# Meta tokens' state update as one product of stacked parts, retention keys in three pieces, and refills two products later, in a hybrid retention and attention block

## The chip, the cores and the metric
One core of a Trainium2 chip runs the kernel. The metric is device time in microseconds of one execution, as the median of the runs. TensorE is called PE, VectorE DVE, ScalarE ACT, GpSimd POOL and SyncE SP.

## The reference
A single encoder block on 1024 tokens of 1024 channels. Sixteen learned meta tokens go in front, so T = 1040. After an RMS norm one product with `w_in` gives the inputs of two branches and their gates:

```python
rq = _rotary(rq); rk = _rotary(rk) * RET_DK ** -0.5        # 4 heads of 128
o_r = _bidirectional_retention(rq, rk, rv, lg_f, lg_b)       # rv: 4 heads of 256
o_r = groupnorm(o_r) * ret_nw * silu(rg);  y_r = o_r @ w_rb
o_a = _windowed_sink_attention(rotary(aq), rotary(ak), av, sink)   # 8 heads, 2 groups
y_a = (o_a * silu(ag)) @ w_ab
mix = sigmoid(gr) * y_r + sigmoid(ga) * y_a
out = h + rms_norm(mix @ w_o)                               # meta tokens dropped
```

Retention works in chunks of 128 tokens. For a chunk c of one head, in one direction:

```python
inner = (q k^T * decay) v                      # inside the chunk
cross = (q * q_decay) @ state                  # what came before
state = chunk_decay * state + (k * k_decay)^T v
```

The meta tokens are a short chunk 0 of 16 tokens: only their state update is needed, in the forward direction.

## The kernel before
**Numbers.** All is in float32 quality: an operand is split into a high and a low part (`..h` and `..l`, of type fp32r), and `mm3` forms a product as three matmuls, high by high (line 76), low by high (77) and high by low (78), summed in one PSUM bank. ACT or POOL copies out the high part, DVE subtracts (`dve_lo`, line 92). The transposed, split input lies in `big`.

**PSUM.** Eight banks in four tags: `pj` has three (projections), `p1` two (transposes `tr` of keys, transposes `to` of outputs), `p2` two (state updates `pkv`), `p3` one (outputs `pa` forward, `pb` backward).

**Setup** (0 to 40 us): the input comes in tile by tile, and the products of head 0 (keys `pk0`, queries `pq0`) follow it in `qk0_mm`. `evac_qk0` rotates them (`rope_evac`: three DVE operations and one POOL addition for each piece).

**Retention** (40 to 330 us), heads 0 to 3. `gen_qk(h)` makes the keys and queries of a head: keys in four `PIECES` of 272, 256, 256, 256 columns, queries in two `HALVES` of 512, each by `proj` (8 k-tiles of `mm3`), then `rope_late` (two DVE multiplications, and two DMAs of POOL that add the swapped halves). It is a generator that yields after each k-tile, so that other code can draw from it by `fill(n)`. `retention(h)` goes over the chunks twice:
- the forward scan: `stage1(c)` projects the values (`pv`, 24 matmuls of 256), splits them into `vh`, `vl` (four buffers each), transposes the keys and forms the scores (tile `tr`), and scales the transposed keys into `khf`, `klf` (forward) and `khb`, `klb` (backward); `stage2(c)` forms the output `pa` (6 matmuls), which ACT and DVE bring to `op`, and the state updates `pkv`: the forward half is added into the state `Sf` on DVE, the backward half is kept by ACT in `kvb`. For chunk 0, all operands have 16 rows, and there is only the forward update, three matmuls of 16 rows.
- the backward scan: for each chunk from 8 to 1 the state `Sb` (DVE) is split (POOL, DVE), `pb` takes three matmuls, DVE adds it to `op` (line 619) and norms it over the 256 channels (lines 623 to 627); `finish` transposes it (`to`, line 595) and ACT copies it out scaled (`ost`, line 600). Between the chunks `fill(KT)` (8 steps) draws the next head's `gen_qk`, 7 times in a head, or in head 3 the keys and values of attention.

**Attention** (330 to 500 us, with the first weights of the later phases), then three **large products** in phases z, r and a: block products by a Strassen-like scheme (seven block products in z and r, with sums T1 to T4 of blocks of the right operand; in a, the sums come from DRAM). `refill` returns, for each numbered place between products, which loads and which splits of the next phase's right operand are issued there.

**Order.** Engines execute in order. The order of instructions is set by the tile scheduler, which takes the program's order and `issue_after` pins and lays the instructions of all engines by its own costs; pools give out buffers and banks in the order of the program.

Of the kernel before, what the change touches and what calls it, by code (L numbers as in the profile page):

```python
# [7 lines left out]
F32 = mybir.dt.float32  # L8
R = mybir.dt.float32r
# [12 lines left out]
SCALE = 128 ** -0.5  # L22
PIECES = [(0, 272), (272, 528), (528, 784), (784, 1040)]
HALVES = [(16, 528), (528, 1040)]
MW = 416
LEFT = 48
FILL = (9, 9, 7, 7, 7, 7, 6, 6), (7,) * 8, (7, 6, 6, 6, 6, 6, 6, 5), (5, 5, 5, 5, 5, 5, 8)
# [12 lines left out]
def block_kernel(ctx: ExitStack, tc: tile.TileContext, x0, xT, x, meta, w_in, w_rb, w_ab, w_out, post_w,  # L40
# [136 lines left out]
    cr = ra.tile([P, T], F32, name="cr")  # L177
    sr = ra.tile([P, T], F32, name="sr")

    def rope_late(t, a, b, o, nm):  # L180

        n = b - a
        m = ra.tile([P, 512], F32, tag="m", bufs=4, name=f"m_{nm}")
        nc.vector.tensor_tensor(m[:, 0:n], t[:, 0:n], sr[:, a:b], ALU.mult)
        nc.vector.tensor_tensor(o[:, 0:n], t[:, 0:n], cr[:, a:b], ALU.mult)
        for r in (0, 64):
            nc.gpsimd.dma_start(o[64 - r:128 - r, 0:n], m[r:r + 64, 0:n], accum_op=ALU.add)

    def rope_evac(t, a, b, o, nm):
        n = b - a  # L190
        m1, m2 = (ra.tile([P, 512], F32, tag="m", bufs=4, name=f"m{i}_{nm}") for i in (1, 2))
        nc.vector.tensor_tensor(m1[:, 0:n], t[:, 0:n], cr[:, a:b], ALU.mult)
        nc.vector.tensor_tensor(m2[64:128, 0:n], t[0:64, 0:n], sr[0:64, a:b], ALU.mult)
        rot = nc.vector.tensor_tensor(m2[0:64, 0:n], t[64:128, 0:n], sr[64:128, a:b], ALU.mult).ins
        nc.gpsimd.tensor_tensor(o[:, 0:n], m1[:, 0:n], m2[:, 0:n], ALU.add)
        return rot


# [53 lines left out]
    def evac_qk0(*pieces):  # L252
        if 0 not in qk:
            qk[0] = [], ra.tile([P, 4, 272], F32, tag="kp", bufs=2, name="kr0")
        q, kt = qk[0]
        for i in pieces:
            m0, a, b, t = (outs[2:] + outs[:2])[i]
            if m0:
                o = kt[:, i]
            else:  # L260
                o = ra.tile([P, 512], F32, tag="q", bufs=6, name=f"qr0_{i}")
                q.append(o)
            rot = rope_evac(t, a, b, o, f"qk0_{i}")
        return rot

    with tc.tile_pool(name="setup", bufs=1, reuse_waits="tile") as st:
# [46 lines left out]
            nc.tensor.matmul(idle[:, 0:KT * (32 + NM)], zeros[:, 0:P], zeros, start=True, stop=True)  # L313


        outs = [(P, a, b, t(f"pk0_{a}")) for (a, b), t in zip(PIECES, (pj, pj, p1, p3))]
        outs = [(0, a, b, p2(f"pq0_{a}")) for a, b in HALVES] + outs

        def qk0_mm(k):
# [53 lines left out]
        first = [projT(wv0, 0, "pv0_0", vmeta0), projT(wv0, 1, "pv0_1"), projT(wv0, 2, "pv0_2")]  # L373
    ra.tile([P, 32], F32, name="space_q")
    with tc.issue_after(rotated):
        turned = evac_qk0(4)
    with tc.issue_after(turned):
        nc.vector.memset(ms, 1.0)
        nc.vector.tensor_scalar(ms[0:NM, 0:1], sumsq[0:NM, 0:1], 1.0 / D, EPS, op0=ALU.mult, op1=ALU.add)
# [61 lines left out]
    def gen_qk(h):  # L441
        w = load_w(w_in, U_QK + h)
        q, kt = [], ra.tile([P, 4, 272], F32, tag="kp", bufs=2, name=f"kr{h}")
        qk[h] = (q, kt)
        for i, (a, b) in enumerate(PIECES):
            t = yield from proj(w, P, a, b, f"pk{h}_{i}")
            rope_late(t, a, b, kt[:, i], f"k{h}_{i}")
            yield
        for i, (a, b) in enumerate(HALVES):
            t = yield from proj(w, 0, a, b, f"pq{h}_{i}")  # L450
            o = ra.tile([P, 512], F32, tag="q", bufs=6, name=f"qr{h}_{i}")
            rope_late(t, a, b, o, f"q{h}_{i}")
            q.append(o)
            yield
# [3 lines left out]
    def retention(h, fill, begin=lambda: None):  # L458
# [21 lines left out]
        def stage1(c):  # L480
            n = NM if c == 0 else P
            pv = first.pop(0) if first else projT(wv, c, f"pv{h}_{c}", vmeta)
            vh = rp.tile([P, 256], R, tag="vh", bufs=4, name=f"vh{h}_{c}")
            vl = rp.tile([P, 256], R, tag="vl", bufs=4, name=f"vl{h}_{c}")
            state["v"] = nc.scalar.copy(vh[0:n], pv[0:n, 0:256]).ins
            state["vl"] = dve_lo(vl[0:n], pv[0:n, 0:256], vh[0:n])
            tr = (p2 if h and c < 2 else p1)(f"tr{h}_{c}")
            nc.tensor.transpose(tr[0:n, 0:P], ksl(c), ident)
            if c > 0:
                nc.tensor.matmul(tr[:, P:2 * P], ksl(c), qs(q, c), start=True, stop=True)  # L490
            kd = {}
            space("space_k", 16)
            for d in ("f", "b"):
                if d == "f" and c > 7 or d == "b" and c < 2:
                    continue
                sc = kd_(h, c, n) if d == "f" else kd_(NH + h, c, n)
                if d == "b":
                    space("space_b", 16)
                a = rp.tile([P, P], R, tag="kh" + d, bufs=2, name=f"kh{d}{h}_{c}")
                b = rp.tile([P, P], R, tag="kl" + d, bufs=2, name=f"kl{d}{h}_{c}")  # L500
                nc.scalar.activation(a[0:n], tr[0:n, 0:P], AF.Copy, scale=sc)
                nc.vector.scalar_tensor_tensor(b[0:n], tr[0:n, 0:P], sc, a[0:n].bitcast(F32), op0=ALU.mult,
                                               op1=ALU.subtract)
                kd[d] = (a, b)
            s = None
            if c > 0:
                sd = rp.tile([P, P], F32, tag="sd", bufs=3, name=f"sd{h}_{c}")
                a = rp.tile([P, P], R, tag="sh", bufs=3, name=f"sh{h}_{c}")
                b = rp.tile([P, P], R, tag="sl", bufs=3, name=f"sl{h}_{c}")
                nc.vector.scalar_tensor_tensor(sd, tr[:, P:2 * P], r2[:, c:c + 1], DT[:, h], op0=ALU.mult, op1=ALU.mult)  # L510
                nc.scalar.copy(a, sd)
                dve_lo(b, sd, a)
                s = (a, b)
            st1[c] = (n, vh, vl, kd, s)
# [9 lines left out]
        def stage2(c):  # L524
            n, vh, vl, kd, s = st1.pop(c)
            if c > 0:
                fh, fl = state["fs"]
                pa = p3(f"pa{h}_{c}")
                mm3(pa[:, 0:256], s[0], s[1], vh, vl, True, True)
                mm3(pa[:, 256:512], qs(qh, c), qs(ql, c), fh, fl, True, True)  # L530
                o = op[c - 1]
                nc.scalar.activation(o, pa[:, 0:256], AF.Copy, scale=rcol[:, c:c + 1])
                nc.vector.scalar_tensor_tensor(o, pa[:, 256:512], qdf(h, c), o, op0=ALU.mult, op1=ALU.add)
            if kd:
                pk = p2(f"pkv{h}_{c}")
            if "f" in kd:
                a, b = kd["f"]
                mm3(pk[:, 0:256], a[0:n], b[0:n], vh[0:n], vl[0:n], True, True)
                new = rp.tile([P, 256], F32, tag="S", bufs=2, name=f"Sf{h}_{c}")
                if c == 0:  # L540
                    nc.vector.tensor_copy(new, pk[:, 0:256])
                else:
                    nc.vector.scalar_tensor_tensor(new, state["f"], cdf(h), pk[:, 0:256], op0=ALU.mult, op1=ALU.add)
                state["f"] = new
                state["fs"] = split_state(new, f"f{h}_{c}")
            if "b" in kd:
                a, b = kd["b"]
                mm3(pk[:, 256:512], a, b, vh, vl, True, True)
                nc.scalar.copy(kvb[c - 1], pk[:, 256:512])
# [56 lines left out]
        for c in range(NB, 0, -1):  # L606
# [25 lines left out]
            if c < 8:  # L632
                with ExitStack() as behind:
                    for p in pins:
                        behind.enter_context(tc.issue_after(p))
                    fill(KT)
            if c == 1:
                begin()
            if c < NB - 1:
# [82 lines left out]
    def gen_ak(g, pieces_=range(4)):  # L722
        if not wak:
            wak.append(load_w(w_in, U_AK))
        for i in pieces_:
            a, b = PIECES[i]
            t = yield from proj(wak[0], P * g, a, b, f"pak{g}_{i}")
            o = rotated_k[g, i] = ra.tile([P, 272], F32, tag="ak", bufs=2, name=f"akr{g}_{i}")
            rope_late(t, a, b, o, f"ak{g}_{i}")
            if not g and i:  # L730
                keys(g, i - 1)
            yield
# [133 lines left out]
    with tc.issue_after(normed):  # L866
        evac_qk0(2)
        decay_table((0,))
        evac_qk0(3, 5)
    heads, drains = [], []  # L870

    def begin_head(h):
# [272 lines left out]
    def refill(nm, src):  # L1145
# [21 lines left out]
            return lambda: get_pre(n)  # L1167

        at = {-16: [load(0, 0)] + ([] if nm == "a" else [load(0, 1)]), -14: [load(1, 1)]}
        each(at, -13, split("B11", 0, 0))  # L1170
        if nm == "a":
            at.update({-11: [got("T1")], -10: [load(1, 0)], -9: [got("T2")], -5: [got("T3")], -1: [got("T4")]})
            each(at, -7, split("B21", 1, 0))
            each(at, -3, split("B22", 1, 1))
            return at
        each(at, -11, minus((0, 0), (0, 1), (0, 0)), split("T1", 0, 0))
        at[-10].append(load(1, 0, range(3)))
        each(at, -7, minus((0, 0), (1, 1), (0, 0)), split("T2", 0, 0))
        each(at, -3, split("B21", 1, 0), minus((0, 0), (1, 0), (0, 0)))
        at[-2].append(load(1, 0, (3,)))  # L1180
        at[1] = at.pop(0)
        each(at, 2, minus((0, 1), (1, 1), (0, 1)))
        each(at, 3, split("T3", 0, 1))
        each(at, 5, split("B22", 1, 1))
        each(at, 7, split("T4", 0, 0))
        return at

    def run(phases):
# [493 lines left out]
```

## Time and profile before
| | |
|---|---|
| median of 3 runs | 1040.86 us (1039.69 to 1041.02) |
| profiled execution | 1040.1 us, its span 1038.3 us |
| PE busy | 1023.7 us, 5883 matmuls |
| DVE busy | 835.8 us, 1802 instructions |
| ACT busy | 502.6 us |
| POOL busy | 228.0 us |
| clock granted to PE | 1.00 in all stretches |

The profile is of one execution. "Busy" is the time in which an engine has an instruction in work; consecutive matmuls overlap in their recorded lengths, so the cost of one in a full queue is the distance from its start to the next start. A view of stretches gives these times for parts of the span; a view of waits tells what an idle engine waited for. All of it is from the kernel before.

### The profile page before, as it was taken

How to read it: one execution, taken by the hardware profiler on the slowest of the kernel's cores; microseconds unless marked ns; L12 is line 12 of the kernel's file. 1: busy time of each engine (PE TensorE's matmuls, PEld its weight loads, DVE VectorE, ACT ScalarE, POOL GpSimd, SP SyncE). 2: the span in 40 equal slices, each digit the busy share in tenths (PEclk: the TensorE clock that was granted, in tenths of full speed). 3: DMA queues.
4: the chain of work that ended last, by engine and by line, in shares of the span. 5: the costliest groups of instructions: out<-in, count | busy, mean ns of one | idle time of the engine just before them, and what ended most of it. 6: DMA issues, size and time to landing. Idle time of an engine off the chain costs nothing. (4 is left out here: it accounts for less than half of the span.)

```text
span 1038.3 us, 17311 instructions
## 1 busy us (share of the span) xinstructions
PE 1023.7 (99%) x5883; PEld 898.0 (86%) x5883; DVE 835.8 (80%) x1802; ACT 502.6 (48%) x1129; POOL 228.0 (22%) x368
## 2 busy tenths in 40 slices
PE   9999999999999999999999999999999999999997
PEld 8998999989989888988888888878888788788886
DVE  7886758768875778778769989999899799778665
ACT  5531432423424566665667554455567446334442
POOL 3445244243342333444310000000000000111032
PEclk9999999999999999999999999999999999999999
DMA  9433123243241466675559679899935746789464
GB/s 357 164 87 88 65 47 84 78 88 104 78 93 62 103 182 189 175 188 161 168 176 326 209 260 338 294 330 365 373 102 178 252 153 226 231 231 325 127 122 81
DMA packets 98840, 188.45 MB, mean 181 GB/s; under 512 B 13024, under 2 KB 37632, under 8 KB 98192
## 3 DMA queue, kind: packets, MB, share of 16 engines
q1 hardware_dynamic: 81200, 162.89, 46.6%
q0 software_dynamic: 10176, 14.73, 9.6%
q10 hardware_dynamic: 7376, 9.73, 2.7%
q8 instruction: 46, 0.75, 0.3%
q14 instruction: 42, 0.34, 0.1%
HBM read 124.32 MB, written 57.68 MB: 175 GB/s over the span
## 5 line engine op out<-in xcount | busy, mean ns | idle before, releaser
L1286 POOL DMA_DIRECT2D mx_d<-c1a x4 | 3.6, 890 | 395.8 <-DVE c1a L1277 377.2
L77 PE MATMUL bz<-big,llz 128*128 128x512 f32 x192 | 74.8, 390 | 0.2 <-DVE llz L92 0.2
L78 PE MATMUL bz<-big,lhz 128*128 128x512 f32 x192 | 74.4, 389 | 0.0
L76 PE MATMUL bz<-big,lhz 128*128 128x512 f32 x192 | 74.0, 390 | 0.3 <-ACT lhz L978 0.3
L76 PE MATMUL pv<-wh,big 128*128 128x256 f32 x256 | 72.8, 284 | 0.0
L77 PE MATMUL pv<-wh,big 128*128 128x256 f32 x256 | 72.7, 284 | 0.0
L78 PE MATMUL pv<-wl,big 128*128 128x256 f32 x256 | 72.7, 284 | 0.0
L76 PE MATMUL bz<-T,lhz 128*128 128x512 f32 x176 | 68.1, 390 | 1.1 <-DVE u2z L1068 1.1
L78 PE MATMUL bz<-T,lhz 128*128 128x512 f32 x176 | 68.5, 389 | 0.0
L77 PE MATMUL bz<-T,llz 128*128 128x512 f32 x176 | 68.5, 389 | 0.0
L76 PE MATMUL paq<-big,wh 128*128 128x512 f32 x128 | 51.6, 403 | 0.0
L1426 ACT ACTIVATE p<-raw,nm 128x337 f32<-128x337 f32 (+1 forms) x64 | 35.5, 556 | 32.2 <-DVE nm L1423 30.6
L77 PE MATMUL paq<-big,wl 128*128 128x512 f32 x128 | 50.2, 392 | 0.0
L78 PE MATMUL paq<-big,wh 128*128 128x512 f32 x128 | 50.2, 392 | 0.0
L1439 POOL TENSOR_SCALAR p<-p,den 128x336 f32<-128x336 f32 (+2 forms) x60 | 34.6, 624 | 66.5 <-DVE den L1430 59.1
L76 PEld LDWEIGHTS pv<-wh,big 128*128 128x128 f32 x256 | 48.3, 189 | 0.4
L77 PEld LDWEIGHTS pv<-wh,big 128*128 128x128 f32 x256 | 48.3, 189 | 0.4
L78 PEld LDWEIGHTS pv<-wl,big 128*128 128x128 f32 x256 | 48.2, 188 | 0.3
L92 DVE TENSOR_TENSOR wl<-wr,wh 128x1024 fp32r<-128x1024 f32 x28 | 35.1, 1258 | 10.4 <-POOL wh L89 6.7
L76 PEld LDWEIGHTS bz<-big,lhz 128*128 128x128 f32 x192 | 36.1, 188 | 8.1 <-ACT lhz L978 0.7
L77 PEld LDWEIGHTS bz<-big,llz 128*128 128x128 f32 x192 | 36.0, 188 | 7.9 <-DVE llz L92 0.5
L78 PEld LDWEIGHTS bz<-big,lhz 128*128 128x128 f32 x192 | 36.0, 188 | 7.5
(621 smaller groups left out, 3594.6 us busy)
## 6 DMA issues: line engine op xcount, KB each, us to landing
wrz<-in_w_in_dram SPq DMA_DIRECT2D x32, 512.0 KB, 6.1
wr<-in_w_in_dram SPq DMA_DIRECT2D x29, 512.0 KB, 4.1
we<-in_w_in_dram SPq DMA_DIRECT2D x16, 512.0 KB, 4.3
tg<-tg_d SPq DMA_DIRECT2D x32, 256.0 KB, 5.1
e<-e ACTq DMA_DIRECT2D x20, 256.0 KB, 2.7
e<-e SPq DMA_DIRECT2D x20, 256.0 KB, 5.3
xn<-in_x_dram SPq DMA_DIRECT2D x8, 512.0 KB, 9.5
oTr_d<-ost SPq DMA_DIRECT2D x16, 256.0 KB, 2.1
```

The source lines that it names most:

```text
L76: nc.tensor.matmul(o, ah, bh, start=first, stop=False, **kw)
L77: nc.tensor.matmul(o, al, bh, start=False, stop=False, **kw)
L78: latest[:] = [nc.tensor.matmul(o, ah, bl, start=False, stop=last, **kw).ins]
L92: return nc.vector.tensor_tensor(o, i, hi.bitcast(F32), ALU.subtract).ins
L1286: nc.gpsimd.dma_start(d, to, accum_op=ALU.add)
L1426: last["exp"] = nc.scalar.activation(pp[:, x_, w0 - o:w0 - o + 1 + wid], r[:, 0:1 + wid], AF.Exp, scale=-1.0, bias=nm_[:, x_:x_ + 1], accu ...
L1439: nc.gpsimd.tensor_scalar(v, v, den[:, x_:x_ + 1], 1.0, op0=ALU.mult, op1=ALU.mult)
```

## The change
Three edits.

1. **Meta state update.** For chunk 0 there is no `vl` and `klf`. `vh` (128 x 256) is cleared by DVE and the 16 rows of the high part of the values are put at rows 0 and 32, the low part at row 64. `khf` (128 x 128) is cleared, and the high part of the keys put at rows 0 and 64, the low part at row 32. One matmul of 128 rows then sums the three products.
2. **Keys in three pieces.** `KEYS` has 272, 256 and 512 columns; the last piece is written to two slots of the key tile through a view of 2 x 256 (`key_piece`, `like`). In head 0 the setup holds one PSUM bank less for keys. The backward scan draws `(9, 5, 6, 6, 6, 8, 8)` steps instead of `8` each in heads 0 to 2, since the three pieces have 8 steps fewer; head 3 is as before. Attention's keys keep `PIECES`.
3. **Refills.** In phases z and r the places of the loads and splits are two products later, up to some that lie one later; phase a is unchanged.

```diff
+KEYS = [(0, 272), (272, 528), (528, 1040)]
...
+    def key_piece(t, i, n):
+        return t[:, 2:4, 0:256] if i == 2 else t[:, i, 0:n]
+
+    def like(t, o):
+        return t.rearrange("p (a c) -> p a c", a=2) if len(o.shape) > 2 else t
...
-        nc.vector.tensor_tensor(o[:, 0:n], t[:, 0:n], cr[:, a:b], ALU.mult)
+        nc.vector.tensor_tensor(o, like(t[:, 0:n], o), like(cr[:, a:b], o), ALU.mult)
         for r in (0, 64):
-            nc.gpsimd.dma_start(o[64 - r:128 - r, 0:n], m[r:r + 64, 0:n], accum_op=ALU.add)
+            nc.gpsimd.dma_start(o[64 - r:128 - r], like(m[r:r + 64, 0:n], o), accum_op=ALU.add)
...
-        outs = [(P, a, b, t(f"pk0_{a}")) for (a, b), t in zip(PIECES, (pj, pj, p1, p3))]
+        outs = [(P, a, b, t(f"pk0_{a}")) for (a, b), t in zip(KEYS, (pj, p1, p3))]
...
-        for i, (a, b) in enumerate(PIECES):
+        for i, (a, b) in enumerate(KEYS):
             t = yield from proj(w, P, a, b, f"pk{h}_{i}")
-            rope_late(t, a, b, kt[:, i], f"k{h}_{i}")
+            rope_late(t, a, b, key_piece(kt, i, b - a), f"k{h}_{i}")
...
-            vl = rp.tile([P, 256], R, tag="vl", bufs=4, name=f"vl{h}_{c}")
-            state["v"] = nc.scalar.copy(vh[0:n], pv[0:n, 0:256]).ins
-            state["vl"] = dve_lo(vl[0:n], pv[0:n, 0:256], vh[0:n])
+            if c:
+                vl = rp.tile([P, 256], R, tag="vl", bufs=4, name=f"vl{h}_{c}")
+                state["v"] = nc.scalar.copy(vh, pv[:, 0:256]).ins
+                state["vl"] = dve_lo(vl, pv[:, 0:256], vh)
+            else:
+                vl = None
+                nc.vector.memset(vh.bitcast(F32), 0.0)
+                for r in (0, 32):
+                    nc.scalar.copy(vh[r:r + n], pv)
+                dve_lo(vh[64:64 + n], pv, vh[0:n])
...
+                if not c:
+                    nc.vector.memset(a.bitcast(F32), 0.0)
+                    for r in (0, 64):
+                        nc.scalar.activation(a[r:r + n], tr[0:n, 0:P], AF.Copy, scale=sc)
+                    nc.vector.scalar_tensor_tensor(a[32:32 + n], tr[0:n, 0:P], sc, a[0:n].bitcast(F32), op0=ALU.mult,
+                                                   op1=ALU.subtract)
+                    kd[d] = a
+                    continue
...
-                a, b = kd["f"]
-                mm3(pk[:, 0:256], a[0:n], b[0:n], vh[0:n], vl[0:n], True, True)
+                if c:
+                    mm3(pk[:, 0:256], *kd["f"], vh, vl, True, True)
+                else:
+                    nc.tensor.matmul(pk[:, 0:256], kd["f"], vh, start=True, stop=True)
...
-                    fill(KT)
+                    fill(KT if h == NH - 1 else (9, 5, 6, 6, 6, 8, 8)[c - 1])
...
-        each(at, -13, split("B11", 0, 0))
+        each(at, -13 if nm == "a" else -11, split("B11", 0, 0))
...
-        each(at, -11, minus((0, 0), (0, 1), (0, 0)), split("T1", 0, 0))
-        at[-10].append(load(1, 0, range(3)))
-        each(at, -7, minus((0, 0), (1, 1), (0, 0)), split("T2", 0, 0))
-        each(at, -3, split("B21", 1, 0), minus((0, 0), (1, 0), (0, 0)))
-        at[-2].append(load(1, 0, (3,)))
-        at[1] = at.pop(0)
-        each(at, 2, minus((0, 1), (1, 1), (0, 1)))
-        each(at, 3, split("T3", 0, 1))
-        each(at, 5, split("B22", 1, 1))
-        each(at, 7, split("T4", 0, 0))
+        each(at, -9, minus((0, 0), (0, 1), (0, 0)), split("T1", 0, 0))
+        at.setdefault(-10, []).append(load(1, 0, range(3)))
+        each(at, -5, minus((0, 0), (1, 1), (0, 0)), split("T2", 0, 0))
+        each(at, -1, split("B21", 1, 0), minus((0, 0), (1, 0), (0, 0)))
+        at[0].append(load(1, 0, (3,)))
+        at[3] = at.pop(2)
+        each(at, 3, minus((0, 1), (1, 1), (0, 1)))
+        each(at, 4, split("T3", 0, 1))
+        each(at, 6, split("B22", 1, 1))
+        each(at, 8, split("T4", 0, 0))
```

More of the change, by code (lines that the diff above doesn't have):

```diff
@@ L194, in rope_evac @@
         rot = nc.vector.tensor_tensor(m2[0:64, 0:n], t[64:128, 0:n], sr[64:128, a:b], ALU.mult).ins
-        nc.gpsimd.tensor_tensor(o[:, 0:n], m1[:, 0:n], m2[:, 0:n], ALU.add)
+        nc.gpsimd.tensor_tensor(o, like(m1[:, 0:n], o), like(m2[:, 0:n], o), ALU.add)
         return rot
@@ L258, in evac_qk0 @@
             if m0:
-                o = kt[:, i]
+                o = key_piece(kt, i, b - a)
             else:
@@ L375, in block_kernel @@
     with tc.issue_after(rotated):
-        turned = evac_qk0(4)
+        turned = evac_qk0(3)
     with tc.issue_after(turned):
@@ L499, in stage1 @@
                 a = rp.tile([P, P], R, tag="kh" + d, bufs=2, name=f"kh{d}{h}_{c}")
+                if not c:
[6 more added lines that the diff above has]
+                    continue
                 b = rp.tile([P, P], R, tag="kl" + d, bufs=2, name=f"kl{d}{h}_{c}")
-                nc.scalar.activation(a[0:n], tr[0:n, 0:P], AF.Copy, scale=sc)
-                nc.vector.scalar_tensor_tensor(b[0:n], tr[0:n, 0:P], sc, a[0:n].bitcast(F32), op0=ALU.mult,
-                                               op1=ALU.subtract)
+                nc.scalar.activation(a, tr[:, 0:P], AF.Copy, scale=sc)
+                nc.vector.scalar_tensor_tensor(b, tr[:, 0:P], sc, a.bitcast(F32), op0=ALU.mult, op1=ALU.subtract)
                 kd[d] = (a, b)
@@ L728, in gen_ak @@
             o = rotated_k[g, i] = ra.tile([P, 272], F32, tag="ak", bufs=2, name=f"akr{g}_{i}")
-            rope_late(t, a, b, o, f"ak{g}_{i}")
+            rope_late(t, a, b, o[:, 0:b - a], f"ak{g}_{i}")
             if not g and i:
@@ L868, in block_kernel @@
         decay_table((0,))
-        evac_qk0(3, 5)
+        evac_qk0(4)
     heads, drains = [], []
```

## The prediction
> **What bounds the kernel now.** I read the page's busy times first, then the stretches of the span, then PE's waits, then the queue of PE instructions by start time.
>
> ```profile
> span 1038.3 us, 17311 instructions
> PE 1023.7 (99%) x5883; PEld 898.0 (86%) x5883; DVE 835.8 (80%) x1802; ACT 502.6 (48%) x1129; POOL 228.0 (22%) x368
> ```
>
> ```profile
> 100.00:170.00 70.00, 70.00 (x534) 66.48 (x534) 52.54 (x146) 23.21 (x70) 28.57 (x44) 1.00 0.27 65
> 240.00:330.00 90.00, 90.00 (x703) 86.50 (x702) 70.59 (x195) 31.68 (x94) 32.52 (x49) 1.00 0.29 77
> 330.00:500.00 170.00, 167.65 (x1012) 148.39 (x1011) 131.73 (x350) 100.47 (x268) 66.03 (x136) 1.00 0.60 162
> 800.00:1038.00 238.00, 229.64 (x1020) 189.17 (x1018) 187.77 (x320) 105.24 (x199) 26.79 (x32) 1.00 0.68 194
> ```
>
> ```profile
> PE ba L77 <- DVE lla L92: 0.9, 1, 0.9
> PE br L77 <- DVE llr L92: 0.8, 2, 0.6
> ```
>
> The stretches give length, then busy time of PE, PE's weight loads, DVE, ACT and POOL, then the granted clock (1.00 throughout). PE is busy 1023.7 of 1038.3 us. In the retention stretches it has no idle time at all; DVE is busy there for 52.54/70 = 75% and 70.59/90 = 78%, ACT for about a third. So in retention the time is the sum of PE's issue intervals: an instruction fewer on PE is worth its interval, and work moved on DVE, ACT or POOL is worth nothing until PE waits for it. The two waits are the only ones over 0.2 us at the starts of phases r and a, where the refills matter.
>
> **Part 1, the meta tokens' state update.** Here the two islands of 16-row matmuls of a head (the lines show start, recorded length, engine, line, operation):
>
> ```profile
> 99.15 0.28 PE L78 MATMUL pv<-wl,big 128*128 128x256 f32 x1
> 99.36 0.38 PE L76 MATMUL pkv<-vh,khf 16*128 16x256 f32 x1
> 99.58 0.27 PE L77 MATMUL pkv<-vh,klf 16*128 16x256 f32 x1
> 99.78 0.38 PE L76 MATMUL pv<-wh,big 128*128 128x256 f32 x1
> 100.00 0.28 PE L77 MATMUL pv<-wh,big 128*128 128x256 f32 x1
> ...
> 100.81 0.28 PE L78 MATMUL pb<-Slb,qh 128*128 128x256 f32 x1
> 101.02 0.38 PE L78 MATMUL pkv<-vl,khf 16*128 16x256 f32 x1
> 101.33 0.39 PE L77 MATMUL pv<-wh,big 128*128 128x256 f32 x1
> 101.55 0.28 PE L78 MATMUL pv<-wl,big 128*128 128x256 f32 x1
> ```
>
> Recorded lengths overlap, so I count from start to start. A full-height 256-wide matmul takes 0.117 here (the key rows below). From 99.15 to 100.00 are four intervals, 0.85 us; without the pair two of 0.117 are left, so the pair costs 0.62. From 100.81 to 101.55 are three intervals, 0.74; two are left, so the single costs 0.51. The three cost 1.12 us, and one 128-row matmul replaces them at 0.117: 1.0 us per head, 4.0 for four heads.
>
> A rule speaks against so much. The Trainium skill, "TensorE: Matmul & The Clock Gate", section "Why this matters for your kernels", says that a single matmul with few contraction rows takes the same time as one with 128; by it only two of three matmuls would go, 8 × 0.117 = 0.94 us. The rows differ: the intervals before, between and behind the 16-row ones are 0.20 to 0.31, not 0.117. The skill's "TensorEngine Tiling (Array Packing)", "Key Properties", has a reason, that changing the tiling drains the engine, and the trace agrees in that the full-height neighbour is late too (101.33 to 101.55).
>
> What it adds, per head: two DVE clears, one more ACT copy of 16x256 and one more ACT scaling of 16x128.
>
> ```profile
> L889 DVE MEMSET vm<- 128x256 f32 x1 | 0.3, 272 | 0.0
> L485 ACT CAST vh<-vmeta 16x256 fp32r<-16x256 f32 x3 | 1.2, 406 | 3.8 <-DVE vmeta L168 3.8
> L501 ACT ACTIVATE khf<-tr,kdr 16x128 fp32r<-16x128 f32 x3 | 1.1, 357 | 0.1
> ```
>
> The 256-wide clear is 0.27 by the first row and the 128-wide one half of that as an estimate, 0.41 together; ACT gets 0.41 + 0.36 = 0.77. Both engines have over 20% free in these stretches and PE goes on with projections meanwhile; the matmul that needs them stands far enough behind in heads 1 to 3. Without cover the two extra ACT operations would stand on the path, at most 0.77 per head.
>
> **Part 2, keys in three pieces.**
>
> ```profile
> 73.47 0.28 PE L76 MATMUL pk<-big,wh 128*128 128x256 f32 x1
> 74.41 0.28 PE L78 MATMUL pk<-big,wh 128*128 128x256 f32 x1
> ...
> 75.23 0.28 PE L76 MATMUL pk<-big,wh 128*128 128x256 f32 x1
> 76.81 0.28 PE L78 MATMUL pk<-big,wh 128*128 128x256 f32 x1
> ...
> 83.81 0.39 PE L76 MATMUL pq<-big,wh 128*128 128x512 f32 x1
> 86.56 0.39 PE L76 MATMUL pq<-big,wh 128*128 128x512 f32 x1
> ```
>
> Between the first two are 8 intervals in 0.94 us, 0.1175 each; between the next two 14 in 1.58, 0.113; between the last two 12 of 512 in 2.75, 0.229. The last two key pieces take 8 × 3 matmuls each per head, so 96 pairs become 96 single ones, in all heads. A pair less a single is 0.235 − 0.229 = +0.006 or 0.226 − 0.229 = −0.003. The gain is between −0.3 and 0.6 us; I take 96 × 0.0047 = 0.45, as most rows are of the slower kind. Rotary multiplications:
>
> ```profile
> L184 DVE TENSOR_TENSOR m_q<-pq,sr 128x512 f32<-128x512 f32 x6 | 4.1, 683 | 2.4 <-PE pq L78 2.4
> L184 DVE TENSOR_TENSOR m_k<-pk,sr 128x256 f32<-128x256 f32 x9 | 3.8, 419 | 0.7 <-PE pk L78 0.7
> ```
>
> Two of 0.68 replace four of 0.42, 0.3 us less DVE per head, and two accumulating DMAs of POOL go; both off PE's path, no gain. The last piece is only ready when its 512 columns are, and its consumers come later than that by several us. In head 0 a PSUM bank less is held in the setup; PE isn't waiting for one there.
>
> **Part 3, refills two products later.** The built instruction streams of the changed kernel with and without this part are the same on every engine, with the same waits and addresses: the tile scheduler orders these operations by its own costs, and the hand-written positions do not decide. So it is 0.0. The two quoted waits of phases r and a stay. Of the queues, SP's keeps 478 instructions and two of them move (the mask load and one store of a head's output); nothing waits for either for tens of us.
>
> **The price: a tighter order in retention.** The back scan of heads 0 to 2 takes 48 steps of the next head's projections instead of 56, and the scheduler lays all of retention anew. I walked the changed PE queue and counted, for each pair of instructions that depend on each other over another engine, the issue intervals between them against the latency from these rows:
>
> ```profile
> 100.12 0.38 PE L595 MATMUL to<-ident,op 128*128 128x128 f32 x2
> 100.54 0.62 ACT L600 ACTIVATE ost<-to,rnw 128x128 f32<-128x128 f32 x2 [2.09 <-PE to L595]
> 101.13 0.48 DVE L619 SCALAR_TENSOR_TENSOR op<-pb,qd,op 128x256 f32<-128x256 f32 x1 [0.73 <-PE pb L78]
> L485 ACT CAST vh<-pv 128x256 fp32r<-128x256 f32 x29 | 10.8, 371 | 14.8 <-PE pv L78 10.8 <-PE pa L77 2.3 <-PE pkv L77 1.7
> L549 ACT COPY kvb<-pkv 128x256 f32<-128x256 f32 x28 | 10.2, 373 | 6.8 <-PE pkv L78 6.8
> L501 ACT ACTIVATE khf<-tr,kdr 128x128 fp32r<-128x128 f32 x28 | 10.3, 368 | 3.5 <-PE tr L490 3.3
> L92 DVE TENSOR_TENSOR vl<-pv,vh 128x256 fp32r<-128x256 f32 x30 | 12.4, 413 | 1.4 <-ACT vh L485 1.1 <-PE pkv L78 0.2
> ```
>
> From the last `pb` matmul's issue (100.81) to its DVE reader are 0.32, and the reader takes 0.48: with a hand-over of 0.06 the bank is free 0.86 after. A copy of ACT instead takes 0.32 + 0.37 + 0.06 = 0.75; an ACT copy with the DVE difference behind it 0.75 + 0.41 + 0.06 = 1.22; a pair of `to` transposes read out by ACT (100.12 to 100.54, then 0.62) about 1.0. Six places of the changed queue have less than that:
>
> - head 0: `pkv_6` follows the backward half of `pkv_4`, in the same bank, after 0.12; 0.75 wanted, 0.6 short.
> - head 1: `pa_1` follows the last `pb_1` of head 0 in the only p3 bank after 0.58; 0.86 wanted, 0.28 short.
> - head 1: `pv_8` needs the bank that the `vh_5`, `vl_5` pair reads, and that pair needs buffers that `pa_1` frees: 0.82 against 1.22, 0.4 short.
> - head 1: `pkv_3` stands 0.65 behind the transposes `tr_3`, `tr_4`; 0.32 + 0.37 + 0.06 and the 0.27 that the product in the same tile issues before ACT may read: 1.0, 0.35 short.
> - head 3: `pb_2`, one transpose pair, `pb_1`: 0.26 against 0.86, 0.6 short.
> - head 3: `to_3`, `to_2`, `to_1` in a row on two banks: 0.33 against 1.0, 0.68 short.
>
> Sum 2.9 us. Stalls of before in this stretch are nil, so the bounds are from afar: nothing (where PE runs late anyway), up to 7.6 (the slower rival). I take 2.9, the plain count.
>
> **The sum.** 1040.1 (profiled execution; span 1038.3, 1.8 around it) − 4.0 − 0.45 + 2.9 = 1038.55. The median of the runs, 1040.86, lies 0.76 above the profiled execution, which would make it 1039.3; I forecast between the two, 1038.9.
>
> **Rivals.**
> *Full gain.* The shortfalls are of 0.3 to 0.7 us each and counted with PE's intervals and single readings of latency; if the queue before each of them runs 0.5 us late, as one stall makes the next one shorter, most vanish. Then 1040.1 − 4.45 = 1035.65, up to 1037.1 with stalls of 1.5. For it: no PE idle at all in the retention of before; against: the two head 3 places, which have no matmul between.
> *Slower: readers queue.* DVE at 75 to 78% executes in order. If at each of the six places the reader stands behind one other DVE or ACT operation (0.48, the `op` row), and in the three that pass through both engines (`vh` and `vl`; `khf`; the `to` read-out with the norm ahead of it) behind an ACT read-out of 0.62 as well, then 6 × 0.48 + 3 × 0.62 = 4.7 us come on top: stalls 7.6, time 1040.1 − 4.45 + 7.6 = 1043.25. It decides from stalls of 4.45 on, 0.74 per place instead of 0.49. For it: DVE's share; against: DVE has less to do than before.
> *Islands not gone.* If the intervals of 0.2 to 0.31 are a wait for the meta operands and not the price of 16 rows, the new matmul meets it as well and only 0.94 of the 4.0 come: 1041.6 with the stalls. Against: the neighbours that need no meta operand are late as well.
> *The refills.* If they did move, 0.9 + 0.8 us of waits could come or go, at most ±1.7. The streams are the same, so no chance is given to it.
>
> **How the numbers follow.** Forecast with stalls between 1.5 and 4.45: 0.50. Full gain 0.27. Islands not gone 0.08. Slower 0.15. What a measurement of this kernel can tell from no change is about 0.2%, 2.1 us, so faster means below 1038.8 and slower above 1042.9. Faster: full gain and under half of the forecast, 0.27 + 0.20 = 0.47. Same: the rest of the forecast, most of the islands case and a part of the slower one, 0.30 + 0.06 + 0.03 = 0.39. Slower: 0.12 and 0.02 from the islands together with queueing, 0.14. The range reaches from the full gain, 1035.6, to 1042.0, which leaves out most of the slower case and little else.
>
> **What would show it.** PE loses 104 instructions (96 + 8); no rows with `16*128 16x256` are left; key rows of 128x512 at 0.229. Retention ends about 1.5 us earlier, with PE idle 2 to 4 us in 40 to 330 where it had none, put down to ACT `kvb`, DVE `op`, DVE `vl`, ACT `khf` and ACT `ost`. The waits for `llr` and `lla` are there as before, moved by the same amount. I am wrong if PE stays at 100% there (full gain), if its idle time is over 4.45 us (slower), or if anything changes by over 1 us behind 330 us.

## The result, and the profile after

| | before | changed |
|---|---|---|
| median of 6 runs | 1040.7 us (1039.09 to 1041.02) | 1045.05 us (1044.07 to 1046.41) |
| ratio | | 1.0047, interval 1.0034 to 1.006 |
| profiled execution, its span | 1040.1, 1038.3 | 1046.35, 1044.6 |

The change makes the kernel 4.35 us slower, 0.47%. 1038.9 was forecast, with a range to 1042.0. The profiled execution of the changed kernel is 1.3 above its median, and that of before 0.6 below its own, so the two profiles lie 6.25 apart where the medians lie 4.35 apart. A second profile of the same instruction streams comes with the third experiment; where a number depends on the execution, both are given.

The page after, its first line and the busy times:

```profile
span 1044.6 us, 17123 instructions
PE 1026.7 (98%) x5779; PEld 894.0 (86%) x5779; DVE 839.3 (80%) x1801; ACT 504.6 (48%) x1137; POOL 226.7 (22%) x361
```

PE has 104 matmuls fewer and is busy 3.0 us longer. The stretches after (length, busy time of PE, its weight loads, DVE, ACT, POOL, then the granted clock):

```profile
100.00:170.00 70.00, 68.76 (x498) 63.99 (x497) 52.70 (x146) 22.93 (x69) 26.72 (x40) 1.00 0.28 67
240.00:330.00 90.00, 89.26 (x690) 85.18 (x689) 74.14 (x202) 29.13 (x88) 34.22 (x52) 1.00 0.27 72
330.00:500.00 170.00, 166.96 (x1016) 147.67 (x1016) 129.81 (x348) 99.55 (x267) 64.17 (x131) 1.00 0.59 159
40.00:330.00 290.00, 287.02 (x2102) 268.78 (x2101) 223.24 (x589) 97.32 (x285) 109.64 (x159) 1.00 0.30 76
```

Retention (40 to 330) now has 2.98 us of idle time on PE, where it had none. What PE waited for after (total, times, longest), of the waits in retention, and at the starts of phases r and a:

```profile
PE pkv L78 <- DVE klf L524: 0.9, 1, 0.9
PE to L618 <- ACT ost L623: 0.6, 1, 0.6
PE pkv L77 <- ACT kvb L572: 0.5, 1, 0.5
PE pb L77 <- DVE op L642: 0.4, 1, 0.4
PE pkv L77 <- ACT khf L523: 0.3, 1, 0.3
PE to L618 <- DVE sd L531: 0.3, 1, 0.3
PE pv L77 <- DVE vl L93: 0.2, 1, 0.2
...
PE ba L78 <- DVE lla L93: 0.9, 1, 0.9
PE br L78 <- DVE llr L93: 0.8, 2, 0.6
```

The releasers are the ones that were named (`kvb`, `op`, `vl`, `khf`, `ost`), and one more kind, `klf` and `sd`. The waits for `lla` and `llr` are as large as before. The islands are gone; here is the stacked matmul of head 0, 0.11 from its neighbours on both sides:

```profile
47.44 0.28 PE L79 MATMUL pv<-wl,big 128*128 128x256 f32 x1
47.55 0.28 PE L561 MATMUL pkv<-vh,khf 128*128 128x256 f32 x1
47.66 0.27 PE L502 MATMUL tr<-ident,kr 128*128 128x128 f32 x1
```

So the mechanisms of the prediction are all in the profile, and yet the sum is off by 6 us. Even the idle time of 2.98 us lies in the 2 to 4 that were forecast, and below the 4.45 that were to tell of the slower case. The next rows, of the `pkv_4` and `pkv_6` place of head 0, show the first reason, how a stall is to be read:

```profile
61.47 0.28 PE L78 MATMUL pkv<-vh,klb 128*128 128x256 f32 x1
61.59 0.28 PE L79 MATMUL pkv<-vl,khb 128*128 128x256 f32 x1
62.33 0.38 PE L77 MATMUL pkv<-vh,khf 128*128 128x256 f32 x1 [0.46 <-ACT kvb L572]
```

Between the last two starts are 0.74 us, 0.62 more than an interval, but the profile shows 0.46 idle: the recorded length of a matmul, 0.28, covers 0.16 beyond its interval. A stall shorter than that is not idle time at all. The Trainium skill, "Perfetto Trace Analysis", section "Tensor Engine Instruction (MATMUL, LD_WEIGHTS)", says that a matmul's end is estimated and not observed; the rows fit that, as the lengths overlap the next start. So stalls are summed here from all starts, from 10 us on up to the first 336-wide `ps` of attention. An interval is compared with those between matmuls of the same two widths; its normal length is the one that a tenth of them stay below. In the trace after, the intervals that are over 0.11 too long sum to 6.8 us in 18 places (6.1 in 13 in the second profile of these streams), before to 1.7 in 7, of which 0.67 are one wait for `aql` and the rest stands at the islands. With the median as the normal length it is 6.5 in 16, 5.9 in 12 and 1.4 in 5. The 2.9 forecast were such a sum of start-to-start distances, so about 6 to 7 stands against it.

One row is used below as a mark, the first 336-wide `ps`, where retention and its end are past. It is the same instruction in all kernels:

```profile
334.00 0.32 PE L76 MATMUL ps<-kTh,aqh 128*128 128x336 f32 x1
```

```profile
338.07 0.31 PE L77 MATMUL ps<-kTh,aqh 128*128 128x336 f32 x1
```

4.1 of the 6.3 us between the profiles lie ahead of it, and 2.2 behind: 1.3 up to the first product of phase z, `bz`, at 546 us, and 0.9 in that phase.

### The profile page after: what moved, and what is told of

Same layout as the page of the kernel before. It is cut to its first block, busy times and chain, and to the rows that moved or that the text cites. A ratio compares the mean times of both kernels' runs of the same rounds, so it can differ in the third digit from the quotient of the medians.

```text
span 1044.6 us, 17123 instructions
## 1 busy us (share of the span) xinstructions
PE 1026.7 (98%) x5779; PEld 894.0 (86%) x5779; DVE 839.3 (80%) x1801; ACT 504.6 (48%) x1137; POOL 226.7 (22%) x361
## 5 line engine op out<-in xcount | busy, mean ns | idle before, releaser
L623 ACT ACTIVATE ost<-to,rnw 128x128 f32<-128x128 f32 x64 | 20.0, 366 | 46.6 <-PE to L618 38.9
```

Of the source, the lines that this page charges most:

```text
L623: nc.scalar.activation(ost[0][:, e_, w0:w0 + P], to[:, P * e_:P * e_ + P], AF.Copy, scale=rnw[:, 2 * h + e_:2 * h + e_ + 1])
```

## The experiments

Runs beside the kernel before on the same chips (its medians there 1040.42 to 1040.53). "Mark" is the start of that `ps` against 334.00:

| run | median | ratio, interval | mark |
|---|---|---|---|
| e1 meta alone | 1040.21 | 0.9996 (0.9987 to 1.0005) | −0.59 |
| e2 keys alone | 1044.80 | 1.0040 (1.0027 to 1.0052) | +3.99 |
| e3 changed, old refill positions | 1044.33 | 1.0034 (1.0022 to 1.0047) | +2.48 |
| e4 before, new refill positions | 1040.44 | 0.9997 (0.9989 to 1.0006) | +0.18 |
| e5 meta alone, vl put back | 1039.35 | 0.9989 (0.9980 to 0.9998) | −1.68 |
| e6 as e5, two banks | 1038.79 | 0.9986 (0.9977 to 0.9995) | −1.96 |
| e7 keys alone, long piece in the middle | 1042.71 | 1.0023 (1.0014 to 1.0032) | +1.90 |
| e8 as e5, keys of head 0 | 1041.31 | 1.0012 (1.0002 to 1.0021) | −2.63 |
| e9 changed, vl put back, two banks | 1043.27 | 1.0029 (1.0017 to 1.0041) | +2.34 |
| e10 as e8, two banks | 1042.58 | 1.0018 (1.0009 to 1.0027) | −2.60 |
| e11 keys alone, two banks | 1045.48 | 1.0050 (1.0038 to 1.0062) | +3.94 |
| e12 before, vl 64 bytes higher | 1041.44 | 1.0009 (1.0000 to 1.0018) | +0.63 |

**e1 and e2: the two parts, each alone.** In e1:

```diff
-KEYS = [(0, 272), (272, 528), (528, 1040)]
+KEYS = PIECES
...
-                    fill(KT if h == NH - 1 else (9, 5, 6, 6, 6, 8, 8)[c - 1])
+                    fill(KT)
```

In e2 the chunk 0 code of before is back:

```diff
-                if c:
-                    mm3(pk[:, 0:256], *kd["f"], vh, vl, True, True)
-                else:
-                    nc.tensor.matmul(pk[:, 0:256], kd["f"], vh, start=True, stop=True)
+                a, b = kd["f"]
+                mm3(pk[:, 0:256], a[0:n], b[0:n], vh[0:n], vl[0:n], True, True)
```

> Only the meta tokens' state update is stacked; keys stay in four pieces and the back scan draws 8 steps each (the refill positions are the changed ones, which leave the streams as they are). Theory A (the gains are there, the places with too little distance in the newly laid PE queue take them back, and both parts together make more such places than either alone): the queue of this kernel has two of the six places, both at the end of head 3, and one of 0.8; minus 4.0 us for the islands, plus about 1.5 for the two places, 0.3 for the third: 1038 us, 2.0 to 3.5 below the kernel before, PE idle in 40 to 330 under 1 us. Theory B (the stacking itself costs: the clears and copies stand on DVE's and ACT's path): slower than before by 3 to 5 us.

> Only the keys are in three pieces, with the drawing of steps that belongs to it; the meta update keeps its three 16-row matmuls. Theory A: minus 0.4 us for the pairs, plus 1.5 for the two places at the end of head 3 and up to 0.5 for others: 1.0 to 1.8 us slower than before, 1042. Theory B: minus 0.4 to 0, as the keys have nothing to do with it. Theory C (the long key piece is the cost, its rotation and its DMAs come late for the transposes): slower by 4 us or more, with PE waiting for kr.

The meta part alone is as fast as before, not 2 to 3.5 us faster; the keys alone are 4.3 slower, as much as the whole change. Theory B (the stacking costs) falls, as e1 isn't slower, and theory A's numbers fail in both. In e1 the 4.0 us of the islands are down to 0.59 at the mark: the two places at the end of head 3 take 1.5 and the new place of `vl` (e5 and e12) about 0.7; the rest isn't accounted for. Three of the waits of PE in retention with the keys alone, early in head 1 (all of them stand with e7):

```profile
120.55 0.44 PE L602 MATMUL to<-ident,op 128*128 128x128 f32 x2 [0.25 <-DVE op L634]
126.59 0.38 PE L77 MATMUL pkv<-vh,khf 128*128 128x256 f32 x1 [0.40 <-ACT khf L508]
127.18 0.38 PE L78 MATMUL pkv<-vh,klf 128*128 128x256 f32 x1 [0.21 <-DVE klf L509]
```

There is no wait for `kr`, the rotated keys. `khf` and `klf` are made from them, but by way of the transposes, and PE doesn't wait at those. That speaks against theory C as it was put; e7 tests it.

**e3 and e4: the refill positions**, e3 with those of before in the changed kernel, e4 with the changed ones in the kernel before, where the first of the lines is:

```diff
-        each(at, -13, split("B11", 0, 0))
+        each(at, -13 if nm == "a" else -11, split("B11", 0, 0))
```

> The changed kernel with the refill positions of before. All theories: the same streams as the changed kernel, so its time within what runs differ, 1044 to 1046.5 us. If the positions did matter, up to 1.7 us either way and other waits for llr and lla.

> The kernel before with only the refill positions changed. All theories: the same streams as before, 1039 to 1041.1 us; a difference between it and before shows what this comparison can't tell.

Both came as expected: e4 is 1040.44 beside 1040.42, e3 within the spread of the changed kernel. The refill part does nothing that these runs can tell. Their marks also show what differs between executions of one stream: 0.18 in e4, but 4.07 and 2.48 in the two of the changed one. Of the 1.6 between those two, 0.7 are in stalls (18 places against 13).

**e7: the same keys in another order.**

```diff
-KEYS = [(0, 272), (272, 528), (528, 1040)]
+KEYS = [(0, 272), (272, 784), (784, 1040)]
```

> The keys part alone with pieces of 272, 512 and 256 columns: the same matmuls, rotations and DMAs as 272, 256, 512, in another order. Theory A (places of the newly laid queue): here pb_1 of head 3 stands 1.19 behind pb_2 instead of 0.26 and pkv_7 of head 3 is no longer short; the ost place of 0.86 stays; two to three stalls in heads 0 to 2 may stay: 1041.5 to 1043. Theory C (three pieces cost by themselves, through the long rotation or fewer, longer matmuls): as the keys part alone, 1044.8.

The same matmuls, rotations and DMAs take 2.1 us less than e2, at the mark as in the time, and every run of e7 is faster than every run of e2. The stalls at `khf` and `klf` in head 1 and at `pb_1` in head 3 are gone. What PE waited for in the two in retention, e2 first:

```profile
PE to L602 <- ACT ost L607: 0.6, 1, 0.6
PE to L602 <- DVE op L634: 0.5, 2, 0.3
PE pb L77 <- DVE op L626: 0.5, 1, 0.5
...
PE pkv L77 <- ACT khf L508: 0.4, 1, 0.4
...
PE pkv L78 <- DVE klf L509: 0.2, 1, 0.2
```

```profile
PE to L602 <- ACT ost L607: 0.6, 1, 0.6
...
PE to L602 <- DVE op L634: 0.4, 1, 0.4
...
PE to L602 <- DVE sd L517: 0.2, 1, 0.2
```

So half of the cost of the keys part hangs on where the newly laid order puts dependent instructions, and not on three pieces as such. That the other half does too is argued from the waits that are left, not shown: no run removes them one by one.

**e5 and e12: an address.** Leaving out `vl` for chunk 0 puts `khf` ahead of `vl` in the pool: `vl` moves from 147776 to 148864 (1024 + 64 bytes), `khf` from 151936 to 147840. In e1, whose queue has few stalls, `pa` matmuls started 118.6 ns apart where they had 116.0, `pkv` 117.6 where they had 116.4 (means of the intervals under 150 ns, which leaves the stalls out). e5 takes a buffer of `vl` for chunk 0 too; e12 moves `vl` by 64 bytes in the kernel before, and nothing else:

```diff
-            if c:
-                vl = rp.tile([P, 256], R, tag="vl", bufs=4, name=f"vl{h}_{c}")
+            vl = rp.tile([P, 256], R, tag="vl", bufs=4, name=f"vl{h}_{c}")
+            if c:
```

```diff
+            space("space_k", 16)
             vl = rp.tile([P, 256], R, tag="vl", bufs=4, name=f"vl{h}_{c}")
```

> The meta part alone, but a vl buffer is also taken for chunk 0 (and left unused), which puts vl, khf and the split key tiles back to the addresses that they have in the kernel before; every engine's order is that of the meta part alone. Theory A2 (the stacking moved vl by 64 bytes against a 256-byte phase, and matmuls that read it, pa and pkv, go 2 to 5 ns slower each): the pa intervals return from 118.5 to 116 ns, all 256-wide ones from 116.5 to 116.1, 0.8 to 1.2 us less than the meta part alone, 1039.2 us. Rival (those intervals are longer for another reason, such as the order): as the meta part alone, 1040.2.

> The kernel before, with nothing changed but the place of the four vl buffers, 64 bytes higher (147840 in place of 147776); order, waits and all other addresses stay. Theory A2 (the phase of vl against its partners in a matmul makes pa and pkv slower): pa intervals from 116.0 to about 118, 0.4 to 0.9 us slower than before, 1040.9 to 1041.3. Rival (khf's new place did it, or the new order): no change, intervals of 116.0.

e5 is 0.86 faster than e1, with `pa` at 116.2; e12 is 0.91 slower than before, with `pa` at 118.3 and `pkv` at 117.8. Both came about as theory A2 has it. As times they are weak: the ratio's interval of e12 just touches no change, and those of e1 and e5 overlap. The distances between starts are the proof: `vl` alone moved in e12, so its place is what lengthens them. The same queue in e12, from the first `pv` of head 0 to the mark (before has its first `pv` at 28.66, e12 at 28.57):

```profile
28.57 0.28 PE L163 MATMUL pv<-wh,xm 128*48 128x256 f32 x1
...
334.63 0.33 PE L76 MATMUL ps<-kTh,aqh 128*128 128x336 f32 x1
```

306.06 us here and 305.34 before, for the same instructions without a new wait: 0.7 us spread over hundreds of matmuls, 1 to 2 ns each. This 0.7 is the part that is shown. Another 0.7 of e12's profile come in phase z, where `vl` isn't read.

**e6, e11 and e9: the end of head 3.** The last backward product and the last transposes get banks of `p2`:

```diff
-                pb = p3(f"pb{h}_{c}")
+                pb = (p2 if h == NH - 1 and c == 1 else p3)(f"pb{h}_{c}")
...
-            to = p1(f"to{h}_{c}")
+            to = (p2 if h == NH - 1 and c == 1 else p1)(f"to{h}_{c}")
```

> As the run before it in this list, and the last backward product and the last output transpose of head 3 take banks of p2 in place of p3 and p1, so that neither waits for the read-out of the one before; the order of the rest stays. Theory A: the two places that cost 0.66 and 0.86 us at 322 to 327 us are gone; the wait for aql of 0.5 to 0.7 that the kernel before has behind them may come back: 0.8 to 1.5 us less than that run, 1037.7 to 1038.4. Rival (something else is late there next): no change.

> The keys part alone with the two banks of p2 at the end of head 3. Theory A: the two places there cost 0.66 and 0.86; the wait for aql behind them may come back: 0.6 to 1.5 less than the keys part alone, 1043.3 to 1044.2. Theory C (three pieces cost by themselves): within 0.4 of it, 1044.4 to 1045.2.

> The changed kernel with vl, khf and the split key tiles back at their old addresses, and the last backward product and last transpose of head 3 in banks of p2; its order is that of the changed kernel but at those two. Theory A adds up: the changed kernel (1044.3 to 1045.1) minus 0.8 for the addresses minus 0.5 to 1.5 for the two places: 1042.2 to 1043.5, still slower than before, with stalls of 2.5 to 4 us left in heads 0 to 2. Rival (these effects belong to the meta part alone and something else covers the same time here): within 0.5 of the changed kernel.

At the mark this brings 0.28 in e6 and 0.05 in e11, not 0.6 to 1.5. The rows of e5 and then e6 say why:

```profile
321.17 0.35 PE L77 MATMUL pb<-Shb,qh 128*128 128x256 f32 x1 [0.45 <-DVE op L641]
325.67 0.44 PE L617 MATMUL to<-ident,op 128*128 128x128 f32 x2 [0.65 <-ACT ost L622]
```

```profile
325.51 0.44 PE L617 MATMUL to<-ident,op 128*128 128x128 f32 x2 [0.66 <-DVE op L649]
```

The wait for the bank of `pb_1` is gone, and that of `to_1` has changed its releaser from ACT's read-out to DVE's norm: with the read-out out of the way, the norm of the same chunk is as late. e11's median is 0.7 above e2's, with intervals that overlap, and in the profiles its loss lies behind the mark. e9 comes to 1043.27, inside theory A's sum, but by luck in part: of the sum, the 0.5 to 1.5 for the two banks didn't come in e6 and e11. It is still 0.29% slower than before. e6 has the lowest median of all kernels, 1038.79, 0.14% below before, with an interval that overlaps that of e5.

**e8 and e10: less retention, no less time.** With `vl` put back and three key pieces in head 0 only, one short place of 0.6 is left.

```diff
-        for i, (a, b) in enumerate(KEYS):
+        for i, (a, b) in enumerate(PIECES):
```

> Meta part with vl put back, and three key pieces in head 0 only (a PSUM bank less in the setup); heads 1 to 3 keep four pieces. Its queue has one short place (pkv_6 of head 0, 0.6) and none at the end of head 3. Theory A: minus 4.0 for the islands, minus 0.1 for 24 pairs, plus 0.6 and up to 0.7 of small ones: 2.5 to 3.4 below before, 1037 to 1038. Theory C: a fourth of the keys' cost stays, 1 us above the first run of this list, 1040.

> Meta part with vl put back, three key pieces in head 0 only, and the two banks of p2 at the end of head 3, where this order has no short place to mend; so nearly the kernel that came out at 1041.3 although its retention ended 2.6 us earlier than that of before. Theory D (attention gives the gain back: ACT waits, in order, for an accumulating DMA of aq that lands late near 485 us, whatever the time at which PE arrives): retention again 2.4 to 2.8 early, attention again 1.5 to 2.5 lost with ACT waiting over 2.5 us for aq, 1041.0 to 1041.5. Rival (one odd profile, the time has another cause): no loss in attention, and the loss elsewhere.

Retention did what theory A said, 2.63 and 2.60 early at the mark. But the times are 1041.31 and 1042.58, over before. In the profiles the gain goes behind the mark: e8 loses 2.1 up to the first `bz` at 546 us and 0.9 in phase z, e10 3.1 and 1.7. The loss in phase z isn't explained. For attention, ACT in e8, then before, at the same instruction:

```profile
485.25 0.62 ACT L691 CAST aqh<-aq 128x512 fp32r<-128x512 f32 x1 [3.25 <-DMA aq<-m_aq]
```

```profile
485.85 0.62 ACT L669 CAST aqh<-aq 128x512 fp32r<-128x512 f32 x1 [1.48 <-DMA aq<-m_aq]
```

ACT waits here for an accumulating DMA of POOL's. ACT was free 2.4 us earlier than before (485.25 less 3.25 against 485.85 less 1.48), but the DMA landed only 0.6 earlier. The softmax on ACT, DVE and POOL follows from there, and PE then waited 1.63 for it at 492.33, where before had no wait at the same transpose. e10 shows the same (its longest wait for `aq` is 3.4), and then something else, in stretches of 2 us (columns as above, the clock is third from the end):

```profile
490.00:492.00 2.00, 1.04 (x9) 0.81 (x7) 1.99 (x7) 0.37 (x1) 2.00 (x5) 1.00 0.21 66
492.00:494.00 2.00, 1.27 (x6) 0.81 (x6) 1.97 (x6) 0.31 (x1) 1.40 (x3) 0.89 0.56 41
494.00:496.00 2.00, 2.00 (x6) 1.57 (x5) 0.87 (x4) 1.96 (x8) 0.82 (x2) 0.50 1.10 301
496.00:498.00 2.00, 2.00 (x8) 1.56 (x8) 1.13 (x3) 0.77 (x1) 0.51 (x3) 0.76 0.46 186
```

PE was busy 2.3 of 4 us, and then the clock was granted at half from 493.56 to 496.97 us: eight 512-wide matmuls started about 0.43 apart instead of 0.23, which costs 1.6 us. The Trainium skill, "TensorE: Matmul & The Clock Gate", section "What's actually happening", has such a halving after an idle window of about 3.4 us; here the waits of PE in sum were 1.7, so the measurement differs. In e8's profile the clock stayed at 1.00, though PE was busy only 1.6 of these 4 us.

The traces say more. In all 14 profiles the changes of the granted clock lie multiples of 3.413 us apart, as on a grid. The step of this grid ahead of the halving, 490.14 to 493.56, has 1.72 us of PE work, the least of any step between 10 us and the last 8 us of all 14 profiles; the next ones, 1.85 in e11 and 1.91 in e8, were followed by the full clock. So the halving seems to hang on how the waits fall into one step; that is a reading of a single case. It isn't rare in e10: 8 of its 12 runs have a mean clock of 0.996 or 0.997, as the profiled one (half of 3.41 us is 0.0016 of the span), with a median of 1043.03 us, the other four 0.998 or 0.999, with 1040.29. In e8 it is 4 of 11 runs (1043.09 against 1041.20) and in e9 2 of 6; the runs of all other kernels here are at 0.998 or 0.999.

Theory D is borne out as to the place and the wait for `aq`, not as to the size: e10 lost 3.1 in attention instead of 1.5 to 2.5, and came out above its range. Why the DMA lands that late stays open.

## Why the prediction was wrong, point by point

- **Islands, 4.0 forecast.** They went: the 28 intervals at the 16-row matmuls took 6.3 us before, and the 20 that are left at 0.113 to 0.118 each take 2.3, so 4.0 went. Right in mechanism and size. The rival by which only 0.94 would come falls.
- **Keys, 0.45 forecast.** The intervals behind the 256- and 512-wide key matmuls summed to 34.34 us before and to 33.94 after: 0.40 (0.60 in e3's profile). Right.
- **Refills, 0.0.** Right (e3, e4).
- **The price of the tighter order, 2.9 forecast.** This is the term that failed. It is 6.1 to 6.8 by the first of the two ways of counting above. Four of the six places are there at about their size: `pkv_6` 0.63 for 0.6, `pa_1` 0.28 for 0.28, `pb_1` 0.69 for 0.6, `to_1` 0.81 for 0.68. `pkv_3` took 0.59 for 0.35. The one at `pv_8` did not stall there; 1.04 is lost beside it at a `pkv` whose `klf` DVE had not made. The other 2 to 3 are in places that the count did not list, such as 0.49 at a `to` behind DVE's `sd`, 0.33 at a `pv` and 0.38 behind transposes. The count took PE's order and single latencies, and left the queues of DVE and ACT to a rival. That rival, "readers queue", with stalls of 7.6 and 1043.25, came nearest, at a chance of 0.15. Its number is partly luck: it put the extra time at the six places, where four came as counted. The sign that was to tell it, idle time over 4.45 us, could not show it either, since idle time leaves out what the recorded lengths cover.
- **A term that was missing.** `vl`'s new address, 0.9 us in the medians of e5 and e12, of which 0.7 are shown in e12's retention. The prediction counted PE's intervals as a property of a matmul's shape.
- **After retention.** That anything there changes by over 1 us was named as a sign of being wrong, and it came: between 1.0 (e3's profile) and 2.2 us (the changed kernel's) came on top. In e8 and e10, whose retention ends early, and in e11, where it ends late, it is 2.1 to 4.9. On the other side, the wait of 0.67 for `aql` at attention's start shrank with PE's later arrival, which the sum did not have.
- **What stays open.** Up to the mark, islands, keys, stalls (less the wait for `aql` of before) and `vl` give +2.4 us for the changed kernel's profile and +1.5 for e3's; 4.07 and 2.48 were measured. The remaining 1 to 1.7 are spread over many intervals that are a little longer, and no run shows why.
- The range ended at 1042.0: it cut off most of the slower rival, and so did not carry the upper bound of 7.6 for a cost that the trace of before could not show.

## What to carry to other kernels

An engine at 100% in the profile is not only a sum of intervals: it is also an order with enough distance between dependent instructions. When a change makes a scheduler lay the order anew, count the distances in the new queue against whole chains with their queues; here the count without them found less than half of the stalls. A gain in one stage is worth what the next stage's slowest arrival lets through. And where code takes or leaves out a buffer, keep the addresses of the others, or measure them.

## What the runs showed of the hardware that was not expected

- Moving one operand tile by 64 bytes, with the same instructions, order and waits, made 256-wide fp32r matmuls of one kind start 118.3 instead of 116.0 ns apart and retention 0.7 us longer (e12); with the tile put back in another kernel, these distances went from 118.6 to 116.2 (e5). What it is about the address was not tried.
- The granted clock can halve for 3.41 us in the middle of a kernel, at a cost of 1.6 us, with no single wait of PE over 1 us: PE was busy 1.72 of the 3.41 us ahead (e10). The clock changes lie on a grid of 3.413 us in all profiles. A stretch as long that lies across that grid, 490.52 to 493.93 in e8, had only 1.05 us of PE work and no halving behind it.
- The recorded length of a 256-wide matmul is 0.28 us where its interval is 0.117, so idle time leaves out 0.16 us of each stall: 2.98 us idle in retention stand beside 6.1 to 6.8 us of lengthened intervals up to the mark.
